# Four pairs of k tiles instead of three in six units of a one-core fp32 encoder block

## The chip, the core and the metric

The kernel runs on one core of a Trainium2 chip. The engines are PE (matmuls; PEld loads its weights), DVE (VectorE), ACT (ScalarE), POOL (GpSimd) and SP, which only issues transfers here. The metric is the device time of one execution in microseconds (us); the time before is a median of three runs. A profile is of one further execution, with times counted from the start of its span. "L744" is line 744 of the kernel before.

## The reference, cut to what matters

One block on 256 tokens of width 2048, in fp32: a gated linear recurrence and a chunked attention, each through a branch product, merged by sigmoid gates; then the output product and a squared-ReLU MLP of width 8192. Cut to the parts that the change touches:

```
z = rms_norm(h) @ w_in
gate_a, gate_b = sigmoid(last 2 x 2048 columns of z)
merged = gate_a * (y_a @ w_branch_a) + gate_b * (y_b @ w_branch_b)
h = h + merged @ w_out
u = rms_norm(h, norm_mlp_w)
h = h + square(relu(u @ w_up)) @ w_down
return rms_norm(h, norm_final_w)
```

## The kernel before

**Products in three matmuls.** Every fp32 operand is split into a high part, rounded to the type fp32r, and a low part, the rest. A product of a left tile (128 k x 128 tokens) and a weight tile (128 k x 512 columns) is three matmuls into one bank of PSUM: high x high, high x low, low x high (mm3, L142). A pair of weight tiles comes as one raw buffer of 512 KB from SP's queue (piece, L672); an ACT cast makes its high part (L89) and a DVE subtraction its low part (L90): this is a split of 128x1024 (parts, L687). There are 8 raw buffers and 6 each for high and low parts (L662); a load can only be issued once the last reader of its buffer is done, and SP issues in order.

**The unit.** gemm_s (L718) is the loop around which all is built. A unit makes 256 tokens (two halves m) x 1024 columns (two halves n of 512) from 16 k tiles, so four banks of 128x512. On r pairs of k tiles, tile k of the first four with tile k + 4, it makes one step of Strassen's method in Winograd's form: 7 products of blocks in place of 8. The left side's four sums S5, S4, S2 and S7 are made once by combos (L615) and serve all units with the same left side; the sums of weight blocks are made by DVE in the raw buffers (add, L740), which are then split again (p1, p3, p5, p2, p6, p7 and p4, in this order). The k tiles beyond the r pairs are plain products ("r" tiles: dn02r1_14 is k tiles 14 and 15 for n = 1 of unit dn02).

With r = 3 the three pairs don't fill whole buffers of two tiles, so two further buffers, X and Y, hold two odd tiles each, loaded by two transfers of 256 KB (L683), with half sums of 128x512 and splits of their own (px, py, px2, p4y). With r = 4 the unit's eight weight buffers are all whole: W12, W11, W22 and W21, two each, loaded in this order (L728 to L738). With r = 2 there are four.

A unit's last plain pair is not done in the unit: it is put into `late` (L888), and the next unit's flush does its matmuls and ends the previous unit's n = 1, after p2 when r is 2 or 3 (L809), or ahead of p5 when r = 4 (L797). The order of one engine's instructions is set by a scheduler that follows the order of the code, and high_priority moves splits, weight sums and evictions ahead of other work.

**Order of units.** ga2, gb0, gb2 (gates, w_in, left side x, sums Sx), then the branch products, wo0 and wo2 (w_out), then four quarters qd of the MLP: up{qd}0, up{qd}2 (w_up, left side h, sums Sh), dn{qd}0, dn{qd}2 (w_down, left side u of that quarter, sums Su). r is 2 in wo2 and up00, 4 in dn of quarters 0 to 2, and 3 elsewhere. For r = 4 combos makes the fourth pair's sums in tokens of the ring ("more", L638) beside the tiles that hold the first three.

**Ends of units.** Gates: ACT's sigmoid into a token. up: ACT's relu and square (L1004, L1005), then PE turns the result into the left side of the down product (turn, L973). dn in quarters 0 to 2: ACT copies the bank into a token y (L1020) and a POOL transfer adds it into h in SBUF (L1021). In the last quarter DVE adds the bank into h (L716), ACT squares it and sums over the row (L1024), and DVE multiplies by the final norm's weight (L1026); the last of the four n then scales by the norm's factor and stores (L1028 to L1039).

**Tokens.** Tiles of 128 x 2 KB in a ring of 17 (TOK, L536) hold the gates, h, relu's results, y, the copies of banks and the sums while they are made.

Of the kernel before, what the change touches and what calls it, by code (L numbers as in the profile page):

```python
# [16 lines left out]
P = 128  # L17
T = 256
NM = T // P
D = 2048  # L20
KD = D // P
FF = 8192
NC = 512
# [27 lines left out]
def tile_hybrid_block(  # L51
# [13 lines left out]
    ps_cms = [tc.tile_pool(name=n, bufs=2, space=PSUM) for n in ("ps_acc", "ps_tp", "ps_sm")]  # L65
    ps_acc, ps_tp, ps_sm = [cm.__enter__() for cm in ps_cms]


    vt = const.tile([P, 48], F32, name="vt")
    nc.scalar.dma_start(vt, cols)  # L70
# [2 lines left out]
    make_identity(nc, ident)  # L73
    ones = const.tile([P, 1], F32, name="ones")
    nc.gpsimd.memset(ones, 1.0)
    warm = const.tile([P, P], F32, name="warm")
    ps_warm = ps_sm.tile([P, P], F32, name="ps_warm", tag="sm")
    with tc.high_priority(offset=10000):
        nc.vector.memset(warm, 0.0)
# [8 lines left out]
    def split(hi, lo, src, copy=None):  # L88
        (copy or nc.scalar.copy)(hi, src)  # L89
        nc.vector.tensor_tensor(lo, src, hi.bitcast(F32), op=ALU.subtract)  # L90
# [92 lines left out]
            nc.vector.tensor_tensor(dst, acc[:, :, 0:T], dst, op=ALU.add)  # L183


    hpool_cm = tc.tile_pool(name="hpool", bufs=1, reuse_waits="tile")
    hp = hpool_cm.__enter__()
# [95 lines left out]
    rstd = const.tile([P, NM], F32, name="rstd")  # L283
    rsqrt(rstd, xsq, D, NM)
    rstd_t = rows(rstd, "rstd")
    rstd8_t = const.tile([P, T], F32, name="rstd8_t")
    nc.vector.tensor_scalar(rstd8_t, rstd_t, 0.125, None, op0=ALU.mult)

    f1, z1 = h2("f1"), h2("zq1")
    add_parts(f1, acc_f1)  # L290
# [209 lines left out]
    a, sc, vs, gws, ends = [None] * 4, [[] for _ in range(4)], [None] * 2, [None] * 2, []  # L500
# [85 lines left out]
    for g in range(2):  # L586
# [10 lines left out]
        for pr in range(5):  # L597
            last = pts
# [5 lines left out]
    def token(what):  # L604
        return tk.tile([P, NC], F32, name=what, tag="t", bufs=TOK)

# [5 lines left out]

    R = 3

    def combos(lhs, what, home, blocks=None, n=R):  # L615

        a = blocks
        if not a:
            a = []
            for m in range(NM):  # L620
                for j in range(2):
                    t = tk.tile([P, R, P], F32, name=f"a{m}{j}_{what}", tag="t", bufs=TOK)
                    x = lhs[j][:, :R, :, m * P:(m + 1) * P].bitcast(F32)
# [12 lines left out]
        for two in ((5, s5), (4, s4)), ((2, s2), (7, s7)):  # L636
            if n > R:
                more = tk.tile([P, 2, 2, P], F32R, name=f"S{two[0][0]}m_{what}", tag="t", bufs=TOK)  # L638
            for q, (i, s) in enumerate(two):
                t = (tk if home == "a" else xp).tile([P, R, 2, P], F32R, name=f"S{i}_{what}", tag=f"S{i}{home}", bufs=1)  # L640
                split(t[:, :, 0, :], t[:, :, 1, :], s[:, :R])
                made[i] = [[t[:, k, u, :] for u in range(2)] for k in range(R)]
# [71 lines left out]
    def evict(dst, acc):  # L714
        with tc.high_priority(offset=2000):
            nc.vector.tensor_tensor(dst, acc, dst, op=ALU.add)  # L716
# [187 lines left out]
    flush()  # L904


# [24 lines left out]
    hT = []  # L931
    Sh = {}

    def h_blocks(n0):
# [33 lines left out]
    for qd in range(NQ):  # L968
        last = qd == NQ - 1
        uT = []  # L970
        pend = []

        def turn(ahead=0):  # L973

            c, rs = pend.pop(0)
            uT.append(new_act(f"u{qd}{c}"))
            hi, lo = uT[-1][:, :, 0, :], uT[-1][:, :, 1, :]
            for m in range(NM):
                tp = transpose4(rs[m], f"u{qd}{c}{m}")
                if c < 2:  # L980
                    blocks[m, c] = tk.tile([P, pairs, P], F32, name=f"a{m}{c}_u{qd}", tag="t", bufs=TOK)
                    nc.scalar.copy(blocks[m, c], tp[:, :pairs])
# [5 lines left out]
        pairs = R if last else 4  # L988

        def turns():  # L990
            if len(hT) == 2:
                h_blocks(2)
            while pend:
                turn()
            if len(uT) == 2:
                Su.update(combos(uT, f"u{qd}", "b", [blocks[m, j] for m in range(NM) for j in range(2)], pairs))

        for c in range(0, 4, 2):
            rs = {}

            def done(m, n, acc, c=c, rs=rs):
                t = token(f"r{qd}{c}")
                with tc.high_priority(offset=2000):
                    nc.scalar.activation(t, acc, AF.Relu, scale=rstd2[:, m:m + 1])  # L1004
                nc.scalar.activation(t, t, AF.Square)  # L1005
                rs[m, n] = t
                if m == NM - 1:
                    pend.append((c + n, [rs[i, n] for i in range(NM)]))

            gemm_s(hT, Sh, w_up, qd * (FF // NQ) + c * NC, f"up{qd}{c}", done, r=R if qd or c else 2, between=turns)  # L1010
        if last:
            wf = apool.tile([P, D], F32, name="wf", tag="act")
            nc.gpsimd.dma_start(wf, bass.AP(tensor=norm_final_w.tensor, offset=norm_final_w.offset, ap=[[0, P], [1, D]]))

        def out_of(m, n, acc, last=last):
            r = h1[n][m]
            if not last:
                t = token(f"y{qd}{n}{m}")
                with tc.high_priority(offset=2000):
                    nc.scalar.copy(t, acc)  # L1020
                nc.gpsimd.dma_start(r, t, accum_op=ALU.add)  # L1021
                return
            evict(r, acc)
            nc.scalar.activation(token(f"ysq_{n}_{m}"), r, AF.Square, accum_out=ssq3[:, m, n:n + 1])  # L1024
            if n < 3:
                nc.vector.tensor_tensor(r, r, wf[:, n * NC:(n + 1) * NC], op=ALU.mult)  # L1026
                return
            nc.vector.tensor_reduce(ssum3[:, m:m + 1], ssq3[:, m, :], axis=AX.X, op=ALU.add)  # L1028
            rsqrt(rstd3[:, m:m + 1], ssum3[:, m:m + 1], D, 1)
            f = rstd3[:, m:m + 1]  # L1030
            for i in range(4):
                t = h1[i][m]
                if i == 3:
                    nc.vector.scalar_tensor_tensor(t, t, f, wf[:, i * NC:(i + 1) * NC], op0=ALU.mult, op1=ALU.mult)
                elif i == 2:
                    nc.vector.tensor_scalar(t, t, f, None, op0=ALU.mult)
                else:
                    nc.scalar.activation(t, t, AF.Copy, scale=f)
                (nc.sync if i % 2 else nc.scalar).dma_start(out[m * P:(m + 1) * P, i * NC:(i + 1) * NC], t)  # L1039

        for n0 in (0, 2):
            gemm_s(uT, Su, w_down, n0 * NC, f"dn{qd}{n0}", lambda m, n, acc, n0=n0: out_of(m, n0 + n, acc), r=pairs, kt0=qd * KD,
                   front=None if n0 else lambda: turn(2000), between=None if n0 else turns, tail=last and n0 == 2)


# [42 lines left out]
```

## Time and profile before

| what | value |
|---|---|
| median of three runs | 1407.68 us (1407.65 to 1408.18) |
| profiled execution: its time | 1407.6 us |
| profiled execution: span in the trace | 1405.9 us |
| granted PE clock over the span | 0.998 |
| DMA | 279.12 MB, mean 199 GB/s |

The span is 1.7 us shorter than the time of the same execution. In the page's rows an engine's busy time stands with its share of the span and the number of its instructions. A row of the timeline gives the start, the duration, the engine, the line and what is written from what is read; in square brackets stands how long the engine was idle before it, and what ended that. A row of the windows gives start and end, the length, and then the busy time of PE, PEld, DVE, ACT and POOL with the number of instructions, PE's granted clock, the DMA engines' share and GB/s.

### The profile page before, as it was taken

Reading aid. Unit: us, or ns where it says so; the run is one execution under the profiler, and the core shown is the slowest. Engines: PE = TensorE matmul, PEld = TensorE weight load, DVE = VectorE, ACT = ScalarE, POOL = GpSimd, SP = SyncE. Lnnn points to the kernel's source line nnn. Section 1 sums busy time; section 2 is a strip of 40 time slices with the busy share of each in tenths; the row PEclk is TensorE's granted clock in tenths of the full one; section 3 lists DMA queues with packets and bytes.
Section 4 is the critical chain, followed back from the end, with each engine's and each line's share of the span. In section 5 each row is a group of like instructions: output and inputs, shape, how many; then the busy total and the mean of one; then the engine's idle time right before and its main releaser. Section 6 shows DMA issues by size and latency. Waiting matters only on the chain.

```text
span 1405.9 us, 18476 instructions
## 1 busy us (share of the span) xinstructions
PE 1393.1 (99%) x6611; PEld 1158.4 (82%) x6611; DVE 1148.5 (82%) x1480; ACT 887.2 (63%) x1191; POOL 55.4 (4%) x116
## 2 busy tenths in 40 slices
PE   9999999999999999999999999999999999999997
PEld 7889888878788888888888888888888888888886
DVE  6898987575768784688998889879997898978984
ACT  6767745464655664445666776667666776668753
POOL 3000001010000000000000000000000000000000
PEclk9999999999999999999999999999999999999999
DMA  9654545555556756656654567764678537787542
GB/s 342 212 180 142 178 146 165 191 166 179 155 179 210 239 197 215 210 172 225 215 193 133 184 233 231 227 216 150 220 245 269 188 129 231 232 269 240 180 154 101
DMA packets 121724, 279.12 MB, mean 199 GB/s; under 512 B 10144, under 2 KB 30624, under 8 KB 121248
## 3 DMA queue, kind: packets, MB, share of 16 engines
q1 hardware_dynamic: 115872, 265.33, 56.5%
q0 software_dynamic: 5040, 11.54, 3.9%
q8 instruction: 52, 0.85, 0.2%
q10 hardware_dynamic: 720, 1.07, 0.2%
q14 instruction: 40, 0.33, 0.1%
HBM read 269.51 MB, written 2.10 MB: 193 GB/s over the span
## 4 chain that ended last, share of the span: by engine, by line
PE 94%; DVE 3%; issue 1%; ACT 1%; DMA 1%; POOL 0%; SPq 0%; POOLq 0%; ACTq 0%; DVEq 0%
PE acc_ak L175 2%; PE acc_aq L175 2%; PE acc_hf L175 2%; PE acc_hq L175 1%; PE ps L393 1%; PE acc_ga L144 1%; PE acc_hg L145 1%; PE acc_hg L143 1%; PE acc_ga L145 1%; PE acc_ba L145 1%; PE acc_hg L144 1%; PE acc_ga L143 1%; PE acc_bb L145 1%; PE acc_av L144 1%; PE acc_av L143 1%; PE acc_bb L143 1%
## 5 line engine op out<-in xcount | busy, mean ns | idle before, releaser
L742 DVE TENSOR_TENSOR raw_dn<-raw_dn,raw_dn 128x1024 f32<-128x1024 f32 x56 | 67.7, 1218 | 0.4
L175 PE MATMUL acc_hq<-act_x,wh_hq 128*128 128x512 f32 x128 | 45.7, 395 | 1.0 <-ACT wh_hq L89 1.0
L175 PE MATMUL acc_aq<-act_x,wh_aq 128*128 128x512 f32 x128 | 46.5, 401 | 0.0
L175 PE MATMUL acc_hf<-act_x,wh_hf 128*128 128x512 f32 x128 | 45.7, 395 | 0.1
L175 PE MATMUL acc_ak<-act_x,wh_ak 128*128 128x512 f32 x128 | 45.0, 397 | 0.0
L742 DVE TENSOR_TENSOR raw_up<-raw_up,raw_up 128x1024 f32<-128x1024 f32 x32 | 39.1, 1222 | 0.7
L1021 POOL DMA_DIRECT2D h<-y x24 | 20.5, 879 | 471.5 <-ACT y L1020 470.9
L174 PE MATMUL acc_hf<-act_x,wl_hf 128*128 128x256 f32 x120 | 34.2, 285 | 0.4 <-DVE wl_hf L90 0.4
L174 PE MATMUL acc_aq<-act_x,wl_aq 128*128 128x256 f32 x120 | 34.6, 288 | 0.0
L90 DVE TENSOR_TENSOR wl_av<-raw_av,wh_av 128x1024 fp32r<-128x1024 f32 x16 | 19.6, 1224 | 18.1 <-ACT wh_av L89 18.1
L174 PE MATMUL acc_hq<-act_x,wl_hq 128*128 128x256 f32 x120 | 34.0, 283 | 0.0
L174 PE MATMUL acc_ak<-act_x,wl_ak 128*128 128x256 f32 x120 | 33.6, 280 | 0.0
L90 DVE TENSOR_TENSOR wl_ba<-raw_ba,wh_ba 128x1024 fp32r<-128x1024 f32 x16 | 19.6, 1224 | 16.6 <-ACT wh_ba L89 16.6
L89 ACT CAST wh_ba<-raw_ba 128x1024 fp32r<-128x1024 f32 x16 | 16.8, 1053 | 24.3 <-PE acc_ba L145 10.0
L90 DVE TENSOR_TENSOR wl_bb<-raw_bb,wh_bb 128x1024 fp32r<-128x1024 f32 x16 | 19.6, 1222 | 14.7 <-ACT wh_bb L89 14.7
L90 DVE TENSOR_TENSOR wl_aq<-raw_aq,wh_aq 128x1024 fp32r<-128x1024 f32 x16 | 19.6, 1224 | 14.4 <-ACT wh_aq L89 14.2
L89 ACT CAST wh_bb<-raw_bb 128x1024 fp32r<-128x1024 f32 x16 | 16.9, 1054 | 22.8 <-PE acc_ba L145 12.8
L89 ACT CAST wh_aq<-raw_aq 128x1024 fp32r<-128x1024 f32 x16 | 16.8, 1048 | 22.2 <-PE acc_hg L145 10.9
L90 DVE TENSOR_TENSOR wl_ga<-raw_ga,wh_ga 128x1024 fp32r<-128x1024 f32 x16 | 19.5, 1224 | 13.7 <-ACT wh_ga L89 13.7
L89 ACT CAST wh_av<-raw_av 128x1024 fp32r<-128x1024 f32 x16 | 16.8, 1052 | 22.0 <-PE acc_av L145 12.4
L89 ACT CAST wh_hg<-raw_hg 128x1024 fp32r<-128x1024 f32 x16 | 16.7, 1045 | 20.8 <-PE acc_hg L145 9.8
L175 PEld LDWEIGHTS acc_hq<-act_x,wh_hq 128*128 128x128 f32 x128 | 24.0, 187 | 6.4 <-ACT wh_hq L89 1.3
(1469 smaller groups left out, 5134.2 us busy)
## 6 DMA issues: line engine op xcount, KB each, us to landing
raw_dn<-in_w_down_dram SPq DMA_DIRECT2D x56, 512.0 KB, 5.8
raw_up<-in_w_up_dram SPq DMA_DIRECT2D x32, 512.0 KB, 7.1
raw_ga<-in_w_in_t_dram SPq DMA_DIRECT2D x20, 512.0 KB, 4.5
raw_hi<-in_w_in_n_dram SPq DMA_DIRECT2D x16, 512.0 KB, 3.9
raw_hg<-in_w_in_n_dram SPq DMA_DIRECT2D x16, 512.0 KB, 3.6
raw_aq<-in_w_in_t_dram SPq DMA_DIRECT2D x16, 512.0 KB, 3.7
raw_ak<-in_w_in_t_dram SPq DMA_DIRECT2D x16, 512.0 KB, 3.7
raw_av<-in_w_in_n_dram SPq DMA_DIRECT2D x16, 512.0 KB, 3.8
```

The lines of the kernel that those rows point to most:

```text
L89: (copy or nc.scalar.copy)(hi, src)
L90: nc.vector.tensor_tensor(lo, src, hi.bitcast(F32), op=ALU.subtract)
L143: nc.tensor.matmul(acc, hi, wh, start=first, stop=False, skip_group_check=True)
L144: nc.tensor.matmul(acc, hi, wl, start=False, stop=False, skip_group_check=True)
L145: nc.tensor.matmul(acc, lo, wh, start=False, stop=last, skip_group_check=True)
L174: nc.tensor.matmul(acc[:, cb, 0:T], wl[:, c], r[:, 0, :], start=False, stop=False)
L175: nc.tensor.matmul(acc[:, cb, :], wh[:, c], r.rearrange("p u t -> p (u t)"), start=kt == 0, stop=kt == nkt - 1)
L393: nc.tensor.matmul(ps[:, m, :], klf[:, a * P:(a + 1) * P], qrf[:, a * 192:(a + 1) * 192], start=True, stop=True)
L742: nc.vector.tensor_tensor(dst, dst, t, op=ALU.add)
L1021: nc.gpsimd.dma_start(r, t, accum_op=ALU.add)
```

## The change

Six units go from r = 3 to r = 4: gb0, gb2, up10, up20, up30 and dn30. What goes with it:

- The sums of the fourth pair of x (Sx) are made by a second call of combos with one k pair (ks, name "x3"), ahead of ga2 in the code; those of h (Sh, "h4") after up00's unit, into a tile Sh4 of their own (4 KB for each partition).
- combos of the last quarter makes four pairs as the other quarters do.
- TOK is 16, not 17; `warm` goes to the pool hp, which is opened earlier, and rstd8_t from the pool of constants to bp, made later.
- In the last quarter n = 0 and 1 (dn30) end as in the other quarters, by a token y and a POOL transfer that adds it into h. Their squares and products with the final norm's weight (weigh) come one unit later, where n = 2 of dn32 ends.

```diff
-    TOK = 17
+    TOK = 16
+    rstd8_t = bp.tile([P, T], F32, name="rstd8_t")
...
-    def combos(lhs, what, home, blocks=None, n=R):
+    def combos(lhs, what, home, blocks=None, n=R, ks=slice(0, R), into=None):
+        nk = ks.stop - ks.start
...
-                    t = tk.tile([P, R, P], F32, name=f"a{m}{j}_{what}", tag="t", bufs=TOK)
-                    x = lhs[j][:, :R, :, m * P:(m + 1) * P].bitcast(F32)
+                    t = tk.tile([P, nk, P], F32, name=f"a{m}{j}_{what}", tag="t", bufs=TOK)
+                    x = lhs[j][:, ks, :, m * P:(m + 1) * P].bitcast(F32)
...
+    for i, s in combos(xT, "x3", "b", ks=slice(R, 4)).items():
+        Sx[i] += s
...
-        gemm_s(xT, Sx, w_in_t, col + c * NC, f"{what}{c}", done, fresh=fresh)
+        gemm_s(xT, Sx, w_in_t, col + c * NC, f"{what}{c}", done, r=R if what == "ga" else 4, fresh=fresh)
...
+    Sh4 = xp.tile([P, 4, 2, P], F32R, name="S_h4")
...
-            gemm_s(hT, Sh, w_up, ..., done, r=R if qd or c else 2, between=turns)
+            gemm_s(hT, Sh, w_up, ..., done, r=R if c else 4 if qd else 2, between=turns)
+            if not qd and not c:
+                for i, s in combos(hT, "h4", None, ks=slice(R, 4), into=[Sh4[:, i:i + 1] for i in range(4)]).items():
+                    Sh[i] += s
...
+        def weigh(m, n):
+            nc.scalar.activation(token(f"ysq_{n}_{m}"), h1[n][m], AF.Square, accum_out=ssq3[:, m, n:n + 1])
+            if n < 3:
+                nc.vector.tensor_tensor(h1[n][m], h1[n][m], wf[:, n * NC:(n + 1) * NC], op=ALU.mult)
...
-            if not last:
+            if last and n > 1:
+                evict(r, acc)
+            else:
                 t = token(f"y{qd}{n}{m}")
                 with tc.high_priority(offset=2000):
                     nc.scalar.copy(t, acc)
                 nc.gpsimd.dma_start(r, t, accum_op=ALU.add)
+            if not last or n < 2:
                 return
-            evict(r, acc)
-            nc.scalar.activation(token(f"ysq_{n}_{m}"), r, AF.Square, accum_out=ssq3[:, m, n:n + 1])
+            if n == 2 and not m:
+                for i in range(2):
+                    for j in range(NM):
+                        weigh(j, i)
+            weigh(m, n)
...
-            gemm_s(uT, Su, w_down, ..., r=pairs, kt0=qd * KD, ...)
+            gemm_s(uT, Su, w_down, ..., r=R if last and n0 else 4, kt0=qd * KD, ...)
```

More of the change, by code (lines that the diff above doesn't have):

```diff
@@ L66, in tile_hybrid_block @@
     ps_acc, ps_tp, ps_sm = [cm.__enter__() for cm in ps_cms]
+    hpool_cm = tc.tile_pool(name="hpool", bufs=1, reuse_waits="tile")
+    hp = hpool_cm.__enter__()
     vt = const.tile([P, 48], F32, name="vt")
@@ L75, in tile_hybrid_block @@
     nc.gpsimd.memset(ones, 1.0)
-    warm = const.tile([P, P], F32, name="warm")
+    warm = hp.tile([P, P], F32, name="warm")
     ps_warm = ps_sm.tile([P, P], F32, name="ps_warm", tag="sm")
@@ L285, in tile_hybrid_block @@
     rstd_t = rows(rstd, "rstd")
-    rstd8_t = const.tile([P, T], F32, name="rstd8_t")
-    nc.vector.tensor_scalar(rstd8_t, rstd_t, 0.125, None, op0=ALU.mult)
     f1, z1 = h2("f1"), h2("zq1")
@@ L535, in tile_hybrid_block @@
     yb = []
-    TOK = 17
+    TOK = 16
+    rstd8_t = bp.tile([P, T], F32, name="rstd8_t")
+    nc.vector.tensor_scalar(rstd8_t, rstd_t, 0.125, None, op0=ALU.mult)
     def qk_chunk(col, what, factor, acc=None):
@@ L639, in combos @@
             for q, (i, s) in enumerate(two):
-                t = (tk if home == "a" else xp).tile([P, R, 2, P], F32R, name=f"S{i}_{what}", tag=f"S{i}{home}", bufs=1)
-                split(t[:, :, 0, :], t[:, :, 1, :], s[:, :R])
-                made[i] = [[t[:, k, u, :] for u in range(2)] for k in range(R)]
+                t = into.pop() if into else (tk if home == "a" else xp).tile([P, R, 2, P], F32R, name=f"S{i}_{what}", tag=f"S{i}{home}", bufs=1)
+                split(t[:, :nk, 0, :], t[:, :nk, 1, :], s[:, :nk])
+                made[i] = [[t[:, k, u, :] for u in range(2)] for k in range(nk)]
                 if n > R:
@@ L980, in turn @@
                 if c < 2:
-                    blocks[m, c] = tk.tile([P, pairs, P], F32, name=f"a{m}{c}_u{qd}", tag="t", bufs=TOK)
-                    nc.scalar.copy(blocks[m, c], tp[:, :pairs])
+                    blocks[m, c] = tk.tile([P, 4, P], F32, name=f"a{m}{c}_u{qd}", tag="t", bufs=TOK)
+                    nc.scalar.copy(blocks[m, c], tp)
                 with tc.high_priority(offset=ahead):
@@ L987, in tile_hybrid_block @@
         blocks = {}
-        pairs = R if last else 4
         def turns():
@@ L995, in turns @@
             if len(uT) == 2:
-                Su.update(combos(uT, f"u{qd}", "b", [blocks[m, j] for m in range(NM) for j in range(2)], pairs))
+                Su.update(combos(uT, f"u{qd}", "b", [blocks[m, j] for m in range(NM) for j in range(2)], 4))
         for c in range(0, 4, 2):
@@ L1008, in done @@
                     pend.append((c + n, [rs[i, n] for i in range(NM)]))
-            gemm_s(hT, Sh, w_up, qd * (FF // NQ) + c * NC, f"up{qd}{c}", done, r=R if qd or c else 2, between=turns)
+            gemm_s(hT, Sh, w_up, qd * (FF // NQ) + c * NC, f"up{qd}{c}", done, r=R if c else 4 if qd else 2, between=turns)
+            if not qd and not c:
+                for i, s in combos(hT, "h4", None, ks=slice(R, 4), into=[Sh4[:, i:i + 1] for i in range(4)]).items():
+                    Sh[i] += s
         if last:
@@ L1041, in tile_hybrid_block @@
         for n0 in (0, 2):
-            gemm_s(uT, Su, w_down, n0 * NC, f"dn{qd}{n0}", lambda m, n, acc, n0=n0: out_of(m, n0 + n, acc), r=pairs, kt0=qd * KD,
+            gemm_s(uT, Su, w_down, n0 * NC, f"dn{qd}{n0}", lambda m, n, acc, n0=n0: out_of(m, n0 + n, acc), r=R if last and n0 else 4, kt0=qd * KD,
                    front=None if n0 else lambda: turn(2000), between=None if n0 else turns, tail=last and n0 == 2)
```

3 lines of the change are left out of this document (removed).

## Prediction

> **What bounds the kernel now.** I read the page first, then the idle time before TensorE, then a table of windows, one for each unit of the product loop that the change touches, and last the single rows around the places that the new instructions reach.
>
> ```profile
> PE 1393.1 (99%) x6611; PEld 1158.4 (82%) x6611; DVE 1148.5 (82%) x1480; ACT 887.2 (63%) x1191; POOL 55.4 (4%) x116
> ...
> PE 94%; DVE 3%; issue 1%; ACT 1%; DMA 1%; POOL 0%; SPq 0%; POOLq 0%; ACTq 0%; DVEq 0%
> ...
> raw_dn<-in_w_down_dram SPq DMA_DIRECT2D x56, 512.0 KB, 5.8
> raw_up<-in_w_up_dram SPq DMA_DIRECT2D x32, 512.0 KB, 7.1
> ```
> ```profile
> PE ps_warm L81 <- DVE warm L79: 1.1, 1, 1.1
> PE acc_hq L175 <- ACT wh_hq L89: 1.0, 1, 1.0
> PE ps L393 <- DVE sd L410: 0.7, 1, 0.7
> PE tpo L479 <- DVE act_ya L482: 0.6, 1, 0.6
> PE acc_hf L174 <- DVE wl_hf L90: 0.4, 1, 0.4
> ```
> PE is busy 99% of the span and holds 94% of the chain that ended last. All that it waits for adds up to 3.8 us, none of it in the units below. So the time is the number of matmuls times their step, and the question for every edit is whether PE stays fed. The step comes from the chain, between the first and the last of 31 consecutive matmuls:
>
> ```profile
> 1379.98 0.23 PE acc_dn32c L145
> ...
> 1386.78 0.23 PE acc_dn32c L145
> ```
> 6.80 us over 30 steps is 0.2267 us. The windows (length, then busy time of PE, PEld, DVE, ACT, POOL) are ga2, gb0, gb2, up02, dn02, up10, up20, up30, dn30:
>
> ```profile
> 418.50:457.90 39.40, 39.35 (x174) 32.24 (x173) 31.72 (x32) 24.27 (x28) 0.00 (x0) 1.00 0.60 201
> 457.90:499.60 41.70, 41.70 (x186) 34.53 (x185) 33.57 (x33) 25.65 (x29) 0.00 (x0) 1.00 0.62 202
> 499.60:541.00 41.40, 41.40 (x184) 34.31 (x183) 29.06 (x27) 25.64 (x29) 0.00 (x0) 1.00 0.75 247
> ...
> 761.40:804.70 43.30, 43.30 (x200) 35.88 (x199) 38.93 (x46) 34.25 (x49) 0.00 (x0) 1.00 0.59 195
> ...
> 847.30:888.10 40.80, 40.80 (x181) 33.78 (x180) 37.00 (x35) 24.74 (x28) 2.55 (x3) 1.00 0.76 232
> 888.10:929.60 41.50, 41.50 (x185) 34.36 (x184) 35.14 (x35) 28.07 (x34) 2.53 (x3) 1.00 0.70 222
> ...
> 1056.40:1097.90 41.50, 41.50 (x185) 34.38 (x184) 33.97 (x34) 27.02 (x32) 2.15 (x3) 1.00 0.69 222
> 1224.60:1266.10 41.50, 41.50 (x184) 34.35 (x183) 33.37 (x33) 27.02 (x32) 2.67 (x4) 1.00 0.77 247
> ...
> 1309.50:1352.80 43.30, 43.30 (x200) 35.86 (x199) 36.25 (x40) 27.81 (x36) 0.00 (x0) 1.00 0.57 194
> ```
> PE fills each window but ga2, at a granted clock of 1.00. DVE is the runner-up. dn02 is what the change wants to make of other units: four pairs already, 180 matmuls, 40.80 us, which is 180 x 0.2267 with no stall, DVE at 37.00.
>
> **The change part by part.** A unit of r pairs issues 192 - 3r matmuls (192 = 16 k tiles x 4 banks x 3), so 183 at r=3 and 180 at r=4. gb0, gb2, up10, up20, up30 and dn30 go from 3 to 4: **6 x 3 = 18 matmuls x 0.2267 = 4.08 us off PE.** The built program has exactly 18 fewer on PE, in these units. The rule from the Trainium skill, TensorE: Matmul & The Clock Gate, section Back-to-back issue gap, has N=512 load-and-matmul pairs at about 131 ns sustained, isolated ones at about 216 ns; 18 would be 2.4 or 3.9 us. The rows here step by 0.2267, and no run here shows 131.
>
> What it costs on the other engines, for each of the six units: a unit at r=4 has 1.5 more splits (an ACT cast and a DVE subtraction of 128x1024) and 8 full weight sums in place of 4 full and 4 half.
>
> ```profile
> 419.03 0.69 DVE L742 TENSOR_TENSOR raw_ga2y<-raw_ga2y,raw_ga2x 128x512 f32<-128x512 f32 x1
> 420.94 1.22 DVE L90 TENSOR_TENSOR wl_ga2p<-raw_ga,wh_ga2p 128x1024 fp32r<-128x1024 f32 x1 [1.23 <-PE acc_ga2c L786]
> 422.20 1.22 DVE L742 TENSOR_TENSOR raw_ga<-raw_ga,raw_ga 128x1024 f32<-128x1024 f32 x1
> ...
> 425.61 1.22 DVE L90 TENSOR_TENSOR wl_ga2px<-raw_ga2x,wh_ga2px 128x1024 fp32r<-128x1024 f32 x1
> ```
> DVE: 1.5 x 1.22 + 4 x 1.22 - 4 x 0.69 = 3.94 us a unit. up10 goes from 35.14 to 39.1 at most, up20 to 37.9, up30 and gb0 to 37.4, gb2 to 33.0, against 40.80 of PE (dn02 holds 37.00 without a stall, so up10 is the new extreme). ACT gains 1.5 casts (about 1.6) and stays under 30. The sum of work fits; what can stall is the order.
>
> The tight order is a unit of four pairs right after another: its eight loads take all eight raw buffers, and the previous unit's last weight pair is split late. dn02 after dn00 shows it (the load of W22's first half landed just before the cast, idle 0.18 for it):
>
> ```profile
> 840.11 1.06 ACT L89 CAST wh_dn02p<-raw_dn 128x1024 fp32r<-128x1024 f32 x1 [0.18 <-DMA raw_dn<-in_w_down_dram]
> ```
> ```profile
> 848.27 1.22 DVE L90 TENSOR_TENSOR wl_dn00r<-raw_dn00r,wh_dn00r 128x1024 fp32r<-128x1024 f32 x1
> ```
> ```profile
> 850.25 0.39 PE L144 MATMUL acc_dn00c<-wl_dn00r,act_u 128*128 128x512 f32 x1
> ```
> From the cast's start to the end of that late split DVE runs 849.49 - 840.11 = 9.38 us back to back; PE wants it 850.25 - 847.30 = 2.95 after the unit's start. So PE is not stalled while W22's load is there 9.38 - 2.95 = 6.43 us ahead of the unit's start; here it was 7.19, slack 0.76. In up10, up20 and up30 the fifth load is Y now and will be W22's first half. Its landing released these rows:
>
> ```profile
> 881.38 0.69 DVE L742 TENSOR_TENSOR raw_up10x<-raw_up10x,raw_up10y 128x512 f32<-128x512 f32 x1 [1.62 <-DMA raw_up10y<-in_w_up_dram]
> ```
> ```profile
> 1048.31 0.69 DVE L742 TENSOR_TENSOR raw_up20x<-raw_up20x,raw_up20y 128x512 f32<-128x512 f32 x1 [0.30 <-DMA raw_up20y<-in_w_up_dram]
> ```
> Ahead of the unit's start that is 888.10 - 881.38 = 6.72 (slack 0.29) and 1056.40 - 1048.31 = 8.09 (slack 1.66); up30 and gb2 I take to be like up20. So up10 alone is near a stall: from 0 (landing as now) to 0.5 (0.8 later); I take **0.1**.
>
> x's fourth sums (12 small DVE operations, 4 of them beside ACT casts) are issued in ga2. They don't exist now; the nearest row is
>
> ```profile
> L90 DVE TENSOR_TENSOR S5m_u<-a_u,S5m_u 128x128 fp32r<-128x128 f32 x6 | 1.7, 282 | 0.0
> ```
> In the built order seven of them stand before the split at 420.94, in front of which DVE idles 1.23, and two more before the px2 split at 425.61, all else from there to 432.05 being back to back. Nine at 0.28 are 2.5 us, less 1.23 is a delay of 1.3 at px2; pipelined at some 0.2 each it is 0.6 or less. That split frees the buffer for the next load, and the load's landing is what ACT waits for here:
>
> ```profile
> 434.10 2.00 ACT L89 CAST wh_ga2r<-raw_ga2r 128x1024 fp32r<-128x1024 f32 x2 [4.38 <-DMA raw_ga2r<-in_w_in_t_dram]
> 436.00 0.58 ACT L772 COPY u_ga<-acc_ga2c 128x512 f32<-128x512 f32 x1
> ```
> ```profile
> 436.19 0.39 PE L145 MATMUL acc_ga2c<-wh_ga2r,act_x 128*128 128x512 f32 x1
> 436.63 0.50 PE L143 MATMUL acc_ga2c<-wh_ga2p,act_x 128*128 128x512 f32 x1
> ```
> The copy of u2 stands behind the two casts, and PE's next matmul starts 0.44 after the one before, not 0.2267: PE stalls here already, so a delay goes straight into the time. Bounds 0 (the landing is set by the other transfers in flight) and 1.3; I take **0.7**, near the middle. The remaining sums fall into the idle 3.14 before 435.18.
>
> h's fourth sums are the same 12 operations in up02: 38.93 + 12 x 0.28 = 42.3 of 43.30, if they don't overlap. They are needed only in up10, three units later, and the splits of weights go ahead of them by priority. At 0.28 each, two at most stand between two splits: 0, or 0.5 if one split is late by that. I take 0.
>
> The last quarter: dn30's first 512 columns (n=0, 1) leave by an ACT copy and a POOL transfer that adds into h (as in quarters 0 to 2), four DVE evictions go, and four squares and four products move into dn32.
>
> ```profile
> L716 DVE TENSOR_TENSOR h<-acc_dn30c,h 128x512 f32<-128x512 f32 x4 | 2.6, 677 | 0.0
> ```
> ```profile
> 1365.04 0.63 ACT L1024 ACTIVATE ysq<-h 128x512 f32<-128x512 f32 x1
> ...
> 1375.31 6.74 ACT L89 CAST wh_dn32r<-raw_dn32r 128x1024 fp32r<-128x1024 f32 x7 [3.06 <-DMA raw_dn32r<-in_w_down_dram]
> 1388.44 0.63 ACT L1024 ACTIVATE ysq<-h 128x512 f32<-128x512 f32 x1 [6.39 <-DVE h L716]
> ```
> ```profile
> DMA to landing us min/median/max: 3.2/3.6/8.8
> ```
> The squares come among the casts from 1376 on, 4 x (0.63 + 0.18 for reading the sum) = 3.2 us, and ACT has 6.39 idle behind these casts: 0. If the cover went, 3.2 would come before the last eviction at most. The transfers land in 3.2 to 8.8 us, and dn30's last copies come near 1365: 2 us of room at worst. From the Trainium skill, SBUF — State Buffer, the box on the "DVE blocks DMA" trap: while DVE runs a 2-port perf-mode operation, GpSimd can't write a POOL-queue transfer's descriptors. By that the squares would wait, and the casts behind them. No row here shows it: the longest landing, 8.8, is with a DVE that the windows of the dn units have at 90%.
>
> Token ring 17 to 16, warm and rstd8_t in other pools, two SP transfers for X and Y fewer per unit: 0. Up to 16 tokens live only at the 16 gates, a ring's worth, and their next users are h1's loads, needed at wo0's eviction long after. The four added transfers meet nothing on POOL's queue before the tail's rstd.
>
> Sum, against the profiled execution (1407.6, the span 1405.9 and 1.7 around it; the median is 0.1 above): 1407.6 - 4.08 + 0.7 + 0.1 = **1404.3 us**.
>
> **The rivals.**
> - *All hidden*: no delay in ga2, none in up10. 1407.6 - 4.1 = 1403.5. For it: dn02, dn12 and dn22 run without a stall. Against: ga2's existing one.
> - *The new pairs starve*: splits in the back-to-back units come late by some tenths each (0.3 to 0.7 in gb2, up10, up20, up30: 1.2 to 2.8 in all), as DVE nears 39.1 of 40.8. 1405.5 to 1407.1, say 1406.0: within 0.2%.
> - *Slower*: W22's landing. w_up's loads take 7.1 us where w_down's take 5.8. If the eight tied buffers make it over 2.0 us later in up10 and over 3.3 in the others, each of the four units loses 1.7: 1404.3 + 6.8 = 1411.1. Point from which it decides: 6.43 us ahead of the unit's start. Against: w_down's units are tied in the same way and have slack.
> - *The transfers of dn30 are late*: if one took 20 us, from 1365, the squares at 1376 and the casts behind them would wait 9, of which ACT's idle 6.39 covers most: 1404.3 + 2.6 = 1406.9, within 0.2%. Against: 24 such transfers landed in 8.8 or less. The box of the Trainium skill above is what could bring it.
> - *It doesn't do what it says*: the built program settles it, 18 matmuls are gone.
>
> **How the numbers follow.** Forecast (1403.9 to 1404.8) 0.42, all hidden 0.24, starving 0.26, W22's landing 0.07, late transfers 0.01. 0.2% of 1407.68 is 2.8 us, about what a measurement can tell from no change: faster below 1404.9. Faster 0.42 + 0.24 = 0.66, same 0.26 + 0.01 = 0.27, slower 0.07. Range: 1403.3 (all hidden, and 0.2 for scatter) to 1406.6 (all but the top of the starving case).
>
> **What would show it.** PE has 18 rows fewer, and the windows of gb0, gb2, up10, up20 and up30 are 0.7 shorter. In ga2 the cast at 434.10 comes about 0.7 later and the step at 436.63 grows by that. The late split's first matmul in up10 starts one step after the one before, or the wait there is the starving case. dn32's squares wait for no transfer. Wrong it is if PE's waits name wl tiles in the six units.

## The result, and the profile after

| | median | runs | ratio to before, 95% interval |
|---|---|---|---|
| before | 1407.85 us | 11 (1407.09 to 1408.33) | |
| changed | 1404.18 us | 11 (1403.64 to 1405.66) | 0.9976 [0.9968, 0.9983] |

Faster by 3.67 us; the interval is 2.4 to 4.5 us. The forecast was 1404.3. The profiled execution took 1403.64 us, its span 1401.8: it is the fastest of the eleven, 0.54 below their median, and compared with the one profiled before it is 3.96 faster.

From the page of the changed kernel: the engines' busy time, and the chain of waits by engine. Line numbers of profiles from here on are those of the kernel that is named.

```profile
PE 1388.8 (99%) x6593; PEld 1154.7 (82%) x6593; DVE 1170.6 (84%) x1510; ACT 899.8 (64%) x1213; POOL 58.2 (4%) x120
...
PE 93%; DVE 3%; issue 1%; ACT 1%; DMA 0%; POOL 0%; SPq 0%; POOLq 0%; ACTq 0%; DVEq 0%
```
6611 - 6593 = 18 matmuls are gone, PE is busy 4.3 us less, DVE 22.1 more and ACT 12.6 more. The windows of the changed kernel, each from a unit's first matmul to the next unit's first: ga2, gb0, up10, up20, up30, dn30 (columns as before):

```profile
418.16:457.81 39.65, 39.36 (x174) 32.15 (x173) 32.82 (x41) 24.85 (x32) 0.00 (x0) 1.00 0.60 200
457.81:498.83 41.02, 41.02 (x182) 33.97 (x181) 36.68 (x34) 27.16 (x30) 0.00 (x0) 1.00 0.61 205
886.73:927.70 40.97, 40.97 (x182) 33.71 (x180) 37.26 (x36) 25.40 (x29) 1.73 (x2) 1.00 0.73 224
1054.47:1095.27 40.80, 40.80 (x181) 33.78 (x180) 37.81 (x36) 27.46 (x32) 1.70 (x2) 1.00 0.72 225
1222.04:1262.84 40.80, 40.80 (x181) 33.78 (x180) 38.23 (x36) 27.35 (x31) 2.29 (x3) 1.00 0.75 250
1306.16:1348.82 42.66, 42.66 (x198) 35.45 (x196) 39.64 (x40) 28.48 (x36) 0.84 (x1) 1.00 0.65 203
```
gb0, up20, up30 and dn30 are 0.64 to 0.70 shorter than in the rows of before; up10 is 0.53 shorter, ga2 0.30 longer (39.35 there from first matmul to first matmul); gb2 with all that follows up to wo0 is 0.69 shorter. So it is six times 0.68, less two small stalls: 3.65 us. The two spans differ by 4.1; most of the rest, 0.35, stands ahead of ga2, whose first matmul starts at 418.16 in place of 418.51. No r changed there, and among all the profiles that start varies by 1.2 us (418.16 to 419.32), so it says nothing of the change. PE's waits have one row that before did not have (line and tile, what released it; total, times, longest):

```profile
PE acc_ga2c L146 <- DVE acc_ga2c L778: 0.3, 1, 0.3
```
Here are the matmuls at that place in the changed kernel, and DVE ahead of them:

```profile
428.36 0.39 PE L148 MATMUL acc_ga2c<-wh_ga2px,S_x 128*128 128x512 f32 x1
429.04 0.50 PE L146 MATMUL acc_ga2c<-wh_ga2r,act_x 128*128 128x512 f32 x1 [0.29 <-DVE acc_ga2c L778]
429.37 0.39 PE L147 MATMUL acc_ga2c<-wl_ga2r,act_x 128*128 128x512 f32 x1
```
```profile
419.29 0.89 DVE L625 TENSOR_TENSOR a_x<-act_x 128x128 f32<-128x128 f32 x4
420.21 0.29 DVE L629 TENSOR_TENSOR a_x<-a_x,a_x 128x128 f32<-128x128 f32 x1
...
421.07 1.22 DVE L93 TENSOR_TENSOR wl_ga2p<-raw_ga,wh_ga2p 128x1024 fp32r<-128x1024 f32 x1
...
428.29 0.69 DVE L778 TENSOR_TENSOR acc_ga2c<-acc_ga2c,s_ga 128x512 f32<-128x512 f32 x1
```
The first seven sums take 419.29 to 421.07, and the splits behind them are late by a fraction of a us. The last of these rows is the addition of s5 into a bank that PE needs next: it ends at 428.98 and PE goes on at 429.04. The steps of 0.68 and 0.33 hold 0.68 + 0.33 - 2 x 0.2267 = 0.56 us of stall. The same addition and the same matmul in the kernel before:

```profile
427.88 0.69 DVE L777 TENSOR_TENSOR acc_ga2c<-acc_ga2c,s_ga 128x512 f32<-128x512 f32 x1
```
```profile
428.94 0.39 PE L143 MATMUL acc_ga2c<-wh_ga2r,act_x 128*128 128x512 f32 x1
```
There the addition ended at 428.57, with 0.37 us to spare. Counted from ga2's first matmul it starts 9.37 us in, and 10.13 in the changed kernel: 0.76 later, twice what there was to spare. The 0.33 us of stall that the kernel before has in ga2 stood 8 us later, behind u2's copy.

In up10 the matmul of the late split starts 0.06 after that split's end. ACT's cast of W22, the split on DVE and PE in the changed kernel:

```profile
880.24 1.06 ACT L92 CAST wh_up10p<-raw_up 128x1024 fp32r<-128x1024 f32 x1 [0.19 <-DMA raw_up<-in_w_up_dram]
```
```profile
888.40 1.22 DVE L93 TENSOR_TENSOR wl_dn02r<-raw_dn02r,wh_dn02r 128x1024 fp32r<-128x1024 f32 x1
```
```profile
889.45 0.39 PE L146 MATMUL acc_dn02c<-wh_dn02r,act_u 128*128 128x512 f32 x1
889.68 0.50 PE L147 MATMUL acc_dn02c<-wl_dn02r,act_u 128*128 128x512 f32 x1
890.01 0.40 PE L148 MATMUL acc_dn02c<-wh_dn02r,act_u 128*128 128x512 f32 x1
```
The cast stands 886.73 - 880.24 = 6.49 us ahead of the unit's start, 0.06 more than the 6.43 that the prediction set, and the slack is 0.06; the step after it is 0.33 in place of 0.2267, a stall of 0.10, with some hundredths behind it: 0.17 in all (40.97 against 40.80). So the rule, which gives no stall here, is good to some 0.2 us.

### The profile page after: what moved, and what is told of

It is laid out like the page before. It is cut to its first block, busy times and chain, and to the rows that moved or that the text cites. A ratio compares the mean times of both kernels' runs of the same rounds, so it can differ in the third digit from the quotient of the medians.

```text
span 1401.8 us, 18485 instructions
## 1 busy us (share of the span) xinstructions
PE 1388.8 (99%) x6593; PEld 1154.7 (82%) x6593; DVE 1170.6 (84%) x1510; ACT 899.8 (64%) x1213; POOL 58.2 (4%) x120
## 4 chain that ended last, share of the span: by engine, by line
PE 93%; DVE 3%; issue 1%; ACT 1%; DMA 0%; POOL 0%; SPq 0%; POOLq 0%; ACTq 0%; DVEq 0%
PE acc_ak L178 2%; PE acc_aq L178 2%; PE acc_hf L178 2%; PE acc_hq L178 1%; PE ps L391 1%; PE acc_hg L148 1%; PE acc_hg L146 1%; PE acc_hg L147 1%; PE acc_ba L148 1%; PE acc_av L146 1%; PE acc_bb L146 1%; PE acc_ba L147 1%; PE acc_bb L147 1%; PE acc_bb L148 1%; PE acc_ba L146 1%
## 5 line engine op out<-in xcount | busy, mean ns | idle before, releaser
L743 DVE TENSOR_TENSOR raw_dn<-raw_dn,raw_dn 128x1024 f32<-128x1024 f32 x60 | 72.5, 1218 | 0.4
L743 DVE TENSOR_TENSOR raw_up<-raw_up,raw_up 128x1024 f32<-128x1024 f32 x44 | 53.4, 1219 | 0.5
L1036 POOL DMA_DIRECT2D h<-y x28 | 24.0, 887 | 593.1 <-ACT y L1035 592.7
```

The lines of the kernel that those rows point to most:

```text
L743: nc.vector.tensor_tensor(dst, dst, t, op=ALU.add)
```

## The experiments

Two theories were on the table. **A**: all that the change costs beside PE is DVE's small sums in ga2 and a landing in up10. **Rivals**: DVE's sum of work starves the new units; the landing of W22 decides; or the last quarter pays. All ratios are to the kernel before, timed on the same chip. Where medians of different groups are compared, those of before agree within 0.12 us (1407.77 to 1407.89).

| run | median us | ratio, 95% interval |
|---|---|---|
| e1_ring | 1408.23 | 1.0002 [0.9993, 1.0011] |
| e2_gates | 1407.04 | 0.9995 [0.9987, 1.0004] |
| e3_up | 1405.94 | 0.9986 [0.9977, 0.9995] |
| e4_dn30 | 1407.26 | 0.9995 [0.9987, 1.0004] |
| e5_x3_between | 1403.87 | 0.9972 [0.9960, 0.9983] |
| e6_s5_behind | 1405.70 | 0.9986 [0.9977, 0.9995] |
| e7_up2_r4 | 1431.84 | 1.0178 [1.0161, 1.0195] |
| e8_dn30_old_end | 1404.40 | 0.9976 [0.9967, 0.9985] |
| e9_w22_late | 1405.61 | 0.9988 [0.9979, 0.9996] |
| e10_dn32_r4 | 1404.74 | 0.9979 [0.9970, 0.9988] |
| e11_turn_ahead | 1420.56 | 1.0092 [1.0076, 1.0107] |
| e12_dve_load | 1404.17 | 0.9974 [0.9964, 0.9984] |

### The change in parts: e1 to e4

Each is the changed kernel with the other parts put back; all four keep the room (TOK 16, the two tiles in other pools).

```diff
# e1_ring: no unit changes its r
# e2_gates: only this
+        gemm_s(xT, Sx, w_in_t, ..., r=R if what == "ga" else 4, fresh=fresh)
# e3_up: only this, with h's fourth sums
+            gemm_s(hT, Sh, w_up, ..., r=R if c else 4 if qd else 2, between=turns)
# e4_dn30: only this, with the last quarter's ends and weigh
+            gemm_s(uT, Su, w_down, ..., r=R if last and n0 else 4, ...)
```

> Only the room: TOK 16, warm and rstd8_t in other pools; r as in the kernel before, the last quarter as before. My account: nothing waits for the seventeenth token, so 0.0 us against before, within 0.4 for scatter, and PE steps as before in ga2 (the 0.44 step of before stays). Rival, that the smaller ring costs something and the six units pay for it: 0.5 us or more slower, with a token's write waiting in the trace.

> The room, and gb0 and gb2 at four pairs with x's fourth sums in ga2; the MLP as before. 6 matmuls x 0.2267 = 1.36 us less on PE. My account after seeing the profile of the changed kernel: ga2's stalls come to 0.56 us in place of before's 0.33, so 1.36 - 0.23 = 1.1 us faster than before. The account on record (0.7 for ga2) gives 0.7 faster, all hidden gives 1.4 faster.

> The room, and up10, up20 and up30 at four pairs with h's fourth sums; gates and last quarter as before. 9 x 0.2267 = 2.04 us less on PE. My account: one stall of 0.1 to 0.2 us in up10 at the split of dn02's last pair, none in up20 and up30, so 1.85 to 1.95 us faster. The starving rival: steps above 0.25 us in each of the three units, 1 us faster or less.

> The room, and dn30 at four pairs with its end by tokens and added transfers and its squares one unit later; the rest as before. 3 x 0.2267 = 0.68 us less on PE and no stall: 0.7 us faster. Rival, that the last quarter pays for the moved squares or waits for a transfer: 0.3 us faster or less, with a wait of ACT for a transfer into h in dn32.

Against the 1407.77 of before in this group the room costs 0.46 us, within its interval (1.0 faster to 1.5 slower), and PE waits for no token in its profile. The gates gain 0.73, w_up's units 1.83 and dn30 0.51: each as expected or 0.2 to 0.4 less. Counted from e1, whose room they share, they are 1.19, 2.29 and 0.97. No single one of these differences is known better than to about 1 us, the intervals of e2 and e4 include no change at all, and the shares of the parts rest on the windows, not on the medians. In e3's profile up10, up20 and up30 are all 40.80 long: no stall even in up10.

e2's profile has ga2 at its worst. The same place as in the changed kernel, and the one that the prediction had in mind:

```profile
428.53 0.39 PE L148 MATMUL acc_ga2c<-wh_ga2px,S_x 128*128 128x512 f32 x1
429.45 0.50 PE L146 MATMUL acc_ga2c<-wh_ga2r,act_x 128*128 128x512 f32 x1 [0.53 <-DVE acc_ga2c L778]
```
```profile
436.86 0.39 PE L148 MATMUL acc_ga2c<-wh_ga2r,act_x 128*128 128x512 f32 x1
437.52 0.50 PE L146 MATMUL acc_ga2c<-wh_ga2p,act_x 128*128 128x512 f32 x1 [0.27 <-ACT u_ga L773]
```
Both stalls are there in one execution: 0.92 - 0.23 at s5's addition, 0.66 - 0.23 at u2's copy, and 0.2 in the steps behind them. Counted from ga2's first matmul, px2's split comes 1.0 us later than before (8.10 in place of 7.10) and the cast that the prediction named 1.06 later (16.65 in place of 15.59), and ga2 is 1.08 longer.

### Are the sums in ga2 the cost, and where: e5 and e6

e5 makes x's fourth sums after p4 of ga2; e6 puts one more DVE operation ahead of s5's addition.

```diff
# e5_x3_between
-    for i, s in combos(xT, "x3", "b", ks=slice(R, 4)).items():
-        Sx[i] += s
+        gemm_s(xT, ..., between=x3 if what == "ga" else None)   # x3: the two lines above
# e6_s5_behind
-        more("12", copy(token(f"s5_{what}"), "22"), ALU.add)
+        s5 = copy(token(f"s5_{what}"), "22")
+        for _ in range(1 if what == "ga2" else 0):
+            nc.vector.tensor_tensor(s5, s5, s5, op=ALU.max)     # high priority
+        more("12", s5, ALU.add)
```

> The changed kernel with x's fourth sums made later in ga2 (after p4, where DVE idles) in place of ahead of ga2 in the code. Theory A, that the changed kernel's stall in ga2 (steps of 0.68 and 0.34 us at 428.4) is DVE's small operations making the addition of s5 late: these steps go back to 0.2267, before's 0.44 step ahead of p4 comes back (0.33 us in all), and the kernel is 0.2 us faster than the changed one, 3.9 us faster than before. Rival, that the stall is from the weight loads' landing: steps of ga2 stay as in the changed kernel.

> The changed kernel with one more DVE operation of 128x512 on s5 in ga2 (s5 = max(s5, s5), nothing changes in value), which puts it and one split of 128x1024 ahead of the addition of s5: that addition starts 0.6 + 1.13 = 1.7 us later. Theory A, that this addition is what PE waits for: the stall there grows by as much, from 0.56 to about 2.3 us, and the kernel is 1.7 us slower than the changed one (2.0 us faster than before). Rival, that the addition has room and the landing decides: no change against the changed kernel.

e5: the stall at s5's addition is gone. PE's matmuls there in e5, with the step back at 0.22 and 0.23:

```profile
428.66 0.39 PE L148 MATMUL acc_ga2c<-wh_ga2px,S_x 128*128 128x512 f32 x1
428.88 0.39 PE L146 MATMUL acc_ga2c<-wh_ga2r,act_x 128*128 128x512 f32 x1
429.11 0.39 PE L147 MATMUL acc_ga2c<-wl_ga2r,act_x 128*128 128x512 f32 x1
```
Its ga2 is 39.15 long. The 0.44 step ahead of p4 that was expected back is not there; the sums don't fall into DVE's idle time either, but between the splits from 435.65 on. One split behind them ends at 438.61, just too late: PE's steps there are 0.27 and 0.33, a stall of 0.14 (in e10, with the same sums, 0.52 and 0.33, a stall of 0.40). Moving the sums takes one stall away and makes a smaller one. Its median is 0.3 below the changed kernel's, as forecast, but the intervals overlap: the trace shows the cause, the times alone would not.

e6: the addition starts at 430.98 and PE waits for it. DVE and PE in e6:

```profile
429.24 0.69 DVE L808 TENSOR_TENSOR s_ga<-s_ga 128x512 f32<-128x512 f32 x1
429.84 1.22 DVE L93 TENSOR_TENSOR wl_ga2r<-raw_ga2r,wh_ga2r 128x1024 fp32r<-128x1024 f32 x1
430.98 0.69 DVE L778 TENSOR_TENSOR acc_ga2c<-acc_ga2c,s_ga 128x512 f32<-128x512 f32 x1
```
```profile
429.40 0.39 PE L147 MATMUL acc_ga2c<-wl_ga2r,act_x 128*128 128x512 f32 x1
431.73 0.72 PE L146 MATMUL acc_ga2c<-wh_ga2r,act_x 128*128 128x512 f32 x1 [1.94 <-DVE acc_ga2c L778]
432.24 0.63 PE L147 MATMUL acc_ga2c<-wl_ga2r,act_x 128*128 128x512 f32 x1
```
DVE's delay of 1.7 us (429.24 to 430.98) costs 1.5 us in the median (1405.70 against 1404.18), known to about 1 us. So at this place DVE's time is the kernel's time.

How large the term is varies from one execution to the next. ga2's length, from its first matmul to gb0's, in the profiles at hand: without the fourth sums 39.35 (before), 39.11 (e1), 39.26 (e3), 38.99 (e4), mean 39.18; with the sums ahead of ga2 39.65 (changed), 40.43 (e2), 39.90 (e7), 39.57 (e8), 39.99 (e9), 39.58 (e11), 39.57 (e12), mean 39.81; made later 39.15 (e5), 39.42 (e10). The sums ahead of ga2 cost 0.6 us. (e6, which delays the addition by design, has 42.84.)

### Is it W22's landing: e9

```diff
# e9_w22_late, up10, up20 and up30 only: load order
-  W12 W12' W11 W11' W22 W22' W21 W21'
+  W12 W12' W11 W11' W22' W21 W22 W21'
```

> The changed kernel with the loads of up10, up20 and up30 in another order: W22's first half is the seventh load of its unit and not the fifth, so it lands some 2.5 us later (two loads of about 1.25 each). In the built order DVE's chain from W22's cast to the late split is one weight sum (1.13) shorter, so PE stalls when W22 lands under 6.43 - 1.13 = 5.3 us ahead of the unit. With landings as in the changed kernel's profile (6.6 ahead in up10, 8.2 in up20, 7.6 in up30) that leaves 4.1, 5.7 and 5.1: stalls of 1.2, 0 and 0.2, in all about 1.4 us slower than the changed kernel (0.3 to 2). Rival, that W22's landing isn't what the late split hangs on: no step above 0.25 us in the three units, no change.

It is 1.4 us slower than the changed kernel, as expected, though the two intervals just overlap. The cast of W22 in up10 of e9, and PE at the late split:

```profile
883.43 1.05 ACT L92 CAST wh_up10p<-raw_up 128x1024 fp32r<-128x1024 f32 x1 [4.14 <-DMA raw_up<-in_w_up_dram]
```
```profile
890.78 0.39 PE L146 MATMUL acc_dn02c<-wh_dn02r,act_u 128*128 128x512 f32 x1
891.60 0.50 PE L147 MATMUL acc_dn02c<-wl_dn02r,act_u 128*128 128x512 f32 x1 [0.43 <-DVE wl_dn02r L93]
```
up10 starts at 888.06, so the cast is 4.63 us ahead; the rule with its 5.3 gives a stall of 0.67, and the two steps hold 0.82 + 0.33 - 0.45 = 0.70. up20 and up30 are 40.80 long: their casts stand 6.6 and 6.3 ahead. So the point from which this rival decides was right, and the changed kernel stands 0.06 us from it in up10 (e5 1.1, e3 1.2). The profile explains only part of the 1.4: up10 is 0.57 longer than in the changed kernel's profile (41.54 against 40.97), where stalls of 1.2, 0 and 0.2 had been expected. Another 0.34 is in ga2, which e9 does not touch. The size of the median is no proof of the rule; the stall is.

### Is it DVE's sum: e12, e7 and e11

e12 adds idle work to DVE; e7 makes three more units of four pairs, which have transposes in them; e11 is e7 with these transposes, their copies and splits put forward.

```diff
# e12_dve_load, second half of up10, up20, up30: four times
+            nc.vector.tensor_tensor(t, src, src, op=ALU.max)       # t: a token, 128x512
# e7_up2_r4
-            gemm_s(hT, Sh, w_up, ..., r=R if c else 4 if qd else 2, between=turns)
+            gemm_s(hT, Sh, w_up, ..., r=4 if qd else R if c else 2, between=turns)
# e11_turn_ahead: e7, and
-                turn()
+                with tc.high_priority(offset=2000):
+                    turn()
```

> The changed kernel with four more DVE operations of 128x512 in the second half of each of up10, up20 and up30 (a scratch token, nothing else reads it): 4 x 0.6 = 2.4 us more DVE in units that hold it at 37.3 to 38.2 of 40.8. It tells DVE's sum from the landings. Theory, that what is tight in a unit of four pairs is the landing of W22 and not DVE's sum: the idle time of DVE takes the 2.4 us up, PE keeps its step in these units, and the time is the changed kernel's within 0.4. Rival, the starving case of the prediction: DVE at 97 to 99% makes splits late by 0.3 to 0.7 us in each of the three units, 1 to 2 us slower than the changed kernel.

> The changed kernel with up12, up22 and up32 at four pairs too: 9 more matmuls gone, 2.04 us less on PE. These units hold DVE at 40.6 of 43.3 us already (the turns), and by the terms of the six units they get some 3.5 us more: 44.1 for 42.6 of PE. Theory, that a unit starves where DVE's sum passes PE's: PE waits about 1.5 us in each for low parts of weights, 4.5 in all, so 2.5 us slower than the changed kernel. Rival, that slack of the neighbouring units takes it up: 2 us faster than the changed kernel, no PE waits.

> The kernel with up12, up22 and up32 at four pairs too (1431.84), and the turns of u (transposes, copies, splits) put ahead of the next unit's first casts by priority. Theory L: what cost 24 us there is a landing, not DVE's sum: the next unit's first weight load comes 5.6 us later than in the changed kernel, its cast stands ahead of the turn's copies in ACT's order, PE's transposes wait behind it, and the clock falls. Then the long waits of the transposes go, and the kernel is below 1415 us, perhaps 1405. Rival S, that DVE's sum of work is the bound: the work is the same, so 1428 to 1435 as before.

e12 takes the same time as the changed kernel. Its windows of up10, up20 and up30:

```profile
887.84:928.64 40.80, 40.80 (x182) 33.78 (x180) 40.12 (x40) 27.10 (x31) 1.72 (x2) 1.00 0.74 225
1055.41:1096.21 40.80, 40.80 (x181) 33.78 (x180) 38.83 (x40) 26.34 (x30) 1.70 (x2) 1.00 0.73 225
1222.98:1263.78 40.80, 40.80 (x181) 33.78 (x180) 38.89 (x40) 26.13 (x30) 2.26 (x3) 1.00 0.76 250
```
In up10 DVE is busy 40.12 of 40.80 us and PE still has no gap; in up20 and up30 it reaches 95% only, as part of the work moved into the next unit. The starving case falls for these units. The added work stands in a unit's second half (911.35 to 917.85 in up10), behind the late split, so e12 tests DVE's sum and not the order ahead of that split, which e9 tests.

e7 is slower by 27.7 us than the changed kernel. Expected were 2.5, so the size is wrong by ten, and the reason too. The largest of PE's waits in e7:

```profile
PE tp_u L109 <- DVE act_u L93: 10.0, 3, 4.4
PE acc_dn10c L147 <- DVE wl_dn10p L93: 1.8, 2, 1.5
```
The first of them, in up12, from ACT, DVE and PE of e7:

```profile
959.46 1.04 ACT L92 CAST wh_dn10p<-raw_dn 128x1024 fp32r<-128x1024 f32 x1 [3.66 <-DMA raw_dn<-in_w_down_dram]
960.41 0.58 ACT L986 COPY a_u<-tp_u 128x512 f32<-128x512 f32 x1
```
```profile
960.53 1.23 DVE L93 TENSOR_TENSOR wl_dn10p<-raw_dn,wh_dn10p 128x1024 fp32r<-128x1024 f32 x1 [3.48 <-ACT wh_dn10p L92]
961.67 1.49 DVE L93 TENSOR_TENSOR act_u<-tp_u,act_u 128x512 fp32r<-128x512 f32 x2
```
```profile
958.86 0.40 PE L146 MATMUL acc_up12c<-wh_up12r,act_h 128*128 128x512 f32 x1
962.41 1.11 PE L109 MATMUL tp_u<-ident,r 128*128 128x128 f32 x4 [3.15 <-DVE act_u L93]
```
DVE is idle for 3.48 us here, so it isn't a bound. All eight buffers are tied, the next unit's first load lands late, its cast stands in ACT's order ahead of the turn's copies, and PE can't transpose the next tile until the last one is read. The waits that e7 adds come to 18.4 us. Behind some of them about 40 matmuls step at some 0.43 us, as the last section shows: an estimate of 40 x 0.2 = 8 us more, in an execution that took 1437.66. e11 puts the turn ahead: the waits of tp_u are gone, and 11.3 of the 27.7 us come back. That is less than was expected (below 1415). What is left is another wait, in e11:

```profile
PE acc_dn10c L148 <- DVE S5m_u L93: 3.4, 1, 3.4
```
u's sums, which have no priority, come behind the splits of dn10 and dn20, with DVE back to back. So in these units the order of turn and cast costs some 11 us. Of the 16.4 us that are left, the waits for u's sums are 7.1 (3.4, 3.2 and 0.5); how the rest divides is left open, and neither the landing alone nor DVE's sum alone explains it.

### The last quarter: e8 and e10

```diff
# e8_dn30_old_end: evict, square and product at once in dn30
-            if last and n > 1:
+            if last:
# e10_dn32_r4: e5, and
-            gemm_s(uT, Su, w_down, ..., r=R if last and n0 else 4, ...)
+            gemm_s(uT, Su, w_down, ..., r=4, ...)
```

> The changed kernel with dn30's end as before: four DVE evictions into h, squares and products at once, no token y and no added transfer; dn30 still at four pairs. My account: dn32's first splits are done 2.9 us or more ahead of PE and get four evictions and four products (0.6 each) among them, two evictions ahead of the tightest: no stall, the same time as the changed kernel within 0.3. Rival, that the squares one unit later are what makes four pairs affordable here: steps above 0.25 us in dn32, 0.5 us or more slower than the changed kernel.

> The changed kernel with x's fourth sums made late in ga2 and dn32 at four pairs too (its sums exist): 3 more matmuls gone, 0.68 us. dn32 has DVE at 34 of 44 us of PE and no transposes, and the last unit loads nothing after it. My account: no stall, 0.7 us faster than the kernel with the late sums alone (1403.87), so 1403.2. Rival, that dn32 right after dn30 ties the buffers as the w_up units after dn units do, with the transposes of the last turn ahead: PE waits in dn30's second half or dn32, and 1404 or more.

e8 takes 0.2 us more than the changed kernel, not to be told from none by the medians. Its profile does have a stall that was not expected: dn32 is 44.23 long in place of 43.97, with two steps of 0.33 (PE starts at 1364.80, 1365.13 and 1365.46) behind a split that ends at 1365.07 and stands behind two of the four evictions. e2 and e3, which also keep the old end, have 44.21 and 44.14 with stalls at other splits, before and e1 43.97; all eight profiles with the new end and dn32 at three pairs have 43.97 or 43.98. So the new end costs nothing that the profiles show; that it saves up to 0.26 us is possible and not shown. In the changed kernel the squares start at 1368.40 without a wait, 8 us after the last transfer's issue:

```profile
1368.40 0.62 ACT L1024 ACTIVATE ysq<-h 128x512 f32<-128x512 f32 x1
```
```profile
1360.78 0.84 POOL L1036 DMA_DIRECT2D h<-y  x1 [0.52 <-ACT y L1035]
```
e10 does shorten dn32, from 43.97 us in e5 (first to last matmul) to 43.29. The median, 1404.74 where 1403.2 was expected, doesn't show it. In its profile up30 is 0.9 longer than 40.80, with one wait:

```profile
1246.71 0.39 PE L148 MATMUL acc_up30c<-wh_up30r,act_h 128*128 128x512 f32 x1
1247.71 0.50 PE L146 MATMUL acc_up30c<-wh_up30p,act_h 128*128 128x512 f32 x1 [0.61 <-ACT u_up L773]
```
It is u2's copy behind a cast that waits for a load, the same form as in ga2 before. e10 doesn't change up30, and the other profiles with up30 at four pairs are 40.80 there, but for e7 and e11, which change the unit behind it; whether this comes more often in e10 is open. No version was shown to beat the changed kernel; e5 has the lowest median.

## Why the prediction was right

- **18 matmuls at 0.2267 us: right.** Six units are shorter by 0.53 to 0.70 us in the profiles, and dn32 in e10 again by 0.68. The sign named for it, 18 rows fewer and windows 0.7 shorter, was there. The steps follow the rows, not the figures of 131 or 216 ns that the Trainium skill gives (TensorE: Matmul & The Clock Gate, section Back-to-back issue gap).
- **ga2, 0.7 us: the size right, the way half right.** The mean over the profiles is 0.6, and in the one execution of the changed kernel it is 0.30. The delay at px2's split, for which the prediction had 0.6 and 1.3, is 0.76 in the changed kernel. The step that failed is "a delay goes straight into the time" by way of the load behind px2. What PE waits for first is s5's addition, which stands two splits behind px2's in the same back-to-back stretch of DVE, and which the prediction never looked at; before, it had 0.37 us to spare (428.57 to PE's 428.94). In the changed kernel the load's cast comes only 0.24 later than before, counted from ga2's first matmul (433.99 and 434.10 on the clocks of the two profiles); PE is later by its 0.56 us of stall already, and the 0.44 step is gone. So the sign named for it, that step growing by 0.7, did not show. e2 shows that both places can stall.
- **up10, 0.1 us: right**, as a term at the edge: 0.17 in the changed kernel's profile, 0 in e3, e5, e6, e7, e8, e10 and e12. The point of 6.43 us gives the slack of the changed kernel (0.06, where the profile has the 0.17), and its form for e9 the stall there to 0.03. "The new extreme" of DVE was not up10: its window holds 37.26 us where 39.1 at most was worked out, and up30's 38.23 where it was 37.4.
- **h's sums, room, squares: nothing, right** (up02, which holds h's sums, is 43.32 long where it was 43.35; e1; e8), the room only to within its interval. The squares come at 1368.40, ahead of the 1376 that was worked out, and still no transfer holds them up.
- **All hidden** (1403.5, 0.24) was the nearest rival; e5 is close to it. It would have been 4.1 us faster, which lies inside the measured interval (2.4 to 4.5): the medians alone don't tell it from the forecast, the longer ga2 in the profiles does. **Starving** falls by the changed kernel's own waits, which name no low part of a weight in the six units, and by e12. **W22's landing** is the right mechanism with some 0.1 us of room in up10 and 1 to 1.5 in the others, and e9 calls it up. **Late transfers**: none was; the landings of the changed kernel are within 9.0 us (8.8 before), those of dn30's four with a median of 6.9. The rule of the Trainium skill (SBUF — State Buffer, the box on the "DVE blocks DMA" trap) is for DVE's 2-port perf-mode operations. The DVE rows beside these four transfers are all TENSOR_TENSOR, and the trace shows no transfer held up.
- The sum was 3.3 us by the terms and 3.67 in the medians, within the interval. That 1404.3 and 1404.18 agree to 0.1 is in part luck: the median of before came out at 1407.85, 0.25 above the execution from which the sum started, and that took up most of the 0.4 by which the terms fall short of the medians' difference.

## What to carry to other kernels

On a kernel with a gapless PE a removed matmul is worth its step, and the whole question is slack: list for each engine what stands behind the inserted work in its order and how long before PE's use it ends, additions into banks as well as splits of weights. A slack written as a rule (a load must be there 6.43 us ahead) can be tested by moving that load, and it tells in advance which unit will stall. The same change in a unit that also holds transposes cost ten times what the sum of work gave, in part (11 of 28 us) since a cast that waits for a late load stands in an engine's order ahead of work that others wait for.

## What the hardware showed that was not expected

In e6's profile the granted clock falls after one gap of 2.33 us between starts of matmuls. A window in e6 that begins just behind the gap, and the one after it:

```profile
432.00:436.00 4.00, 4.00 (x12) 3.09 (x12) 2.69 (x6) 0.09 (x1) 0.00 (x0) 0.59 0.99 344
436.00:461.00 25.00, 25.00 (x112) 20.69 (x111) 17.77 (x16) 14.09 (x15) 0.00 (x0) 1.00 0.54 188
```
The steps are 0.427 us in place of 0.2267 for some 3 us, about 1.6 us lost. That execution took 1407.35 us where the median is 1405.70. Of the ten, only this one and one of 1407.16 show a clock of 0.997 over the span, so most executions of the same kernel don't pay it. In e7 the same steps of 0.427 follow the stall of 3.55 us (from 965.03 on), and they also follow three shorter waits in a row (1.13, 1.50 and 0.65 us between 988.50 and 993.17); its clock over the span is 0.988. In e11 three waits of 1.13, 0.76 and 0.52 us between 1329.19 and 1333.91 are followed by none. So these profiles give no single length of gap from which the clock falls.
